# Attention features projected in pairs: seven block products, half of K ahead of the delta heads and half behind them

## The chip, the cores and the metric

One core of one Trainium2 chip runs the kernel. The metric is the device time of one execution in microseconds (us), the median of several runs. Five engines work side by side, each through its own list of instructions in a fixed order: TensorE (PE; its weight loads are shown apart as PEld), VectorE (DVE), ScalarE (ACT), GpSimd (POOL) and SyncE (SP), which only issues loads and stores. An instruction starts when the one before it on its engine is done with and when the semaphores it waits for have come.

## The reference

One encoder layer over 768 tokens, 512 of a prompt and 256 of a sample, which share the weights but do not see each other. The model width is 2048, and everything is float32.

```python
h = rms_norm(x, norm_g)
proj = h @ w_in            # 8192 features and 32 small columns
aq, ak, av, ag, dq, dk, dv, dg, b_raw, a_raw = split(proj)
attn = dilated_attention(aq, ak, av) * silu(ag)          # 8 heads x 128
qkv = silu(short_conv(concat(dq, dk, dv)))               # five taps over the tokens
dn = rms_norm(delta(fwd) + delta(bwd)) * silu(dg)        # 8 heads x 128
y = rms_norm(x + concat(attn, dn) @ w_out, final_gain)
```

Half of the 64 tiles of 128 features (`aq`, `ak`, `av`, `ag`) belong to attention, the other half to the delta heads. Each head of attention needs its q, k and v whole; each delta head its convolved q, k and v.

## The kernel before

**Exact products.** Float32 products are made from short parts: a tile `w` is split into `hi` (a cast on ScalarE) and `lo = w - hi` (a subtraction on VectorE or GpSimd; `w_split`, line 304), x likewise (`x_split`, line 401). A product is then hi·xh + hi·xl + lo·xh, three matmuls with the same shapes into one PSUM bank.

**Input projection.** `project` (line 470) does one tile of 128 features for all tokens: 16 K tiles, three products, each as a matmul of 512 prompt columns and one of 256 sample columns (`kstep`, line 321). The 64 tiles make 6144 matmuls `mm`. The x in them is not normalised: rows of x carry only the gain, and each tile's result is multiplied by `rB`, the reciprocal root mean square of every token, as it leaves PSUM. So the first product needs the first K tile of x, and not the mean over all of them. `x_squares` (line 411) adds the squares of x up, thirteen of the sums on GpSimd, and `start_rms` (line 554) makes `rB` by two matmuls `rms` with a matrix of ones. Beside the first tile run the small columns a and b (`ab_step`).

**Order.** Engines run written lists. A `Driver` makes them when the kernel is built: it keeps a rough clock of each engine, emits the projection's products one after the other, and after each product offers a place (`slot`, line 171) for up to three steps of side tasks whose inputs are due by those clocks. Delta heads (`prep`, `merge`, `chain`, `head_out`) and attention heads (`attend`, line 1007) are such side tasks; `drain` emits whatever side tasks are left, with nothing between them. Feature tiles come in this order: q, k, v of the delta heads with their gates, then q, k, v of each attention head with its gate behind it. The last four gates of attention (`LATE = 4`) stand behind the last head's q, k and v, so that products are left to go between the steps of the last heads.

**One head of attention.** `attend` works by 128 queries: S (scores, three matmuls per query tile), a VectorE row that adds the table of biases and takes the maximum, exp on ScalarE, the scaling on VectorE, transposes T, a split into high and low parts on ScalarE and VectorE, and at the end the product o with V. Prompt (four query tiles of 512 keys) and sample (two of 256) follow each other, and heads follow each other.

**Output projection.** The mixed features go through DRAM (`mixD`), are loaded back and split (`m_load`, `m_splits`), and multiplied with `w_out` in matmuls `mmo` of 512 columns (`ostep`).

The profile names lines of helpers: 192 is every instruction of VectorE, ScalarE and GpSimd, 272 every matmul, 277 every transpose, 234 every load and store.

## Time and profile before

| | |
|---|---|
| median of 3 runs | 1665.43 us (1664.51 to 1665.91) |
| span of the profiled execution, first to last instruction | 1662.0 us |
| PE busy | 1615.9 us, 97% |
| DVE, ACT, POOL busy | 841.0, 736.3, 416.3 us |
| mean granted clock of TensorE | 0.995 |
| moved by DMA | 150.32 MB |

The profiled execution is known by its span; its time as the runs count it is not listed. The median lies 3.4 us above the span, and by that much a span is brought to a time below. Busy times of PE count modelled ends of pipelined matmuls, so the pace of matmuls is read from start to start. "Idle before" is what an engine stood still ahead of an instruction, and the name behind the arrow is what it waited for.

### The profile page before, as it was taken

Reading aid. Unit: us, or ns where it says so; the run is one execution under the profiler, and the core shown is the slowest. Engines: PE = TensorE matmul, PEld = TensorE weight load, DVE = VectorE, ACT = ScalarE, POOL = GpSimd, SP = SyncE. Lnnn points to the kernel's source line nnn. Section 1 sums busy time; section 2 is a strip of 40 time slices with the busy share of each in tenths; the row PEclk is TensorE's granted clock in tenths of the full one; section 3 lists DMA queues with packets and bytes.
Section 4 is the critical chain, followed back from the end, with each engine's and each line's share of the span. In section 5 each row is a group of like instructions: output and inputs, shape, how many; then the busy total and the mean of one; then the engine's idle time right before and its main releaser. Section 6 shows DMA issues by size and latency. Waiting matters only on the chain.

```text
span 1662.0 us, 27562 instructions
## 1 busy us (share of the span) xinstructions
PE 1615.9 (97%) x10283; PEld 1392.2 (84%) x10283; DVE 841.0 (51%) x1956; ACT 736.3 (44%) x1861; POOL 416.3 (25%) x430
## 2 busy tenths in 40 slices
PE   5999999999999999999999999999999999999997
PEld 4788788888888888898888888888888888888885
DVE  6758674857677767675343342425334336313132
ACT  5575546564765566553433232424333335202121
POOL 4443413232424242332121222222121210111100
PEclk9999999999999999999999999999999999999999
DMA  5232312232323232313212222221221256534365
GB/s 190 61 89 72 97 47 79 64 87 59 83 62 87 65 80 65 87 47 84 67 49 79 65 61 69 61 75 55 78 75 57 72 188 224 158 91 118 90 200 180
DMA packets 107783, 150.32 MB, mean 90 GB/s; under 512 B 40864, under 2 KB 48128, under 8 KB 107648
## 3 DMA queue, kind: packets, MB, share of 16 engines
q1 hardware_dynamic: 105632, 143.83, 29.8%
q10 hardware_dynamic: 2016, 4.72, 0.7%
q8 instruction: 81, 1.33, 0.3%
q14 instruction: 54, 0.44, 0.1%
HBM read 125.65 MB, written 22.86 MB: 89 GB/s over the span
## 4 chain that ended last, share of the span: by engine, by line
PE 78%; DVE 9%; DMA 5%; ACT 4%; issue 3%; SPq 1%; POOL 0%; DVEq 0%; POOLq 0%; ACTq 0%
PE mm L272 55%; PE mmo L272 11%; PE c L272 5%; DVE lop L192 2%; PE o L272 2%; PE S L272 2%; DMA res<-in_x 1%; PE m L272 1%; DVE tmp L192 1%; PE kk L272 1%; PE T L277 1%; DMA xst<-in_xT 1%; DVE cacc L192 1%; DMA st<-in_wt 1%; DVE PB L192 1%
## 5 line engine op out<-in xcount | busy, mean ns | idle before, releaser
L272 PE MATMUL mm<-xl_x,hip 128*128 128x512 f32 (+1 forms) x2048 | 541.4, 345 | 7.6 <-DVE xl_x L192 7.6
L272 PE MATMUL mm<-xh_x,hip 128*128 128x512 f32 (+1 forms) x2048 | 538.0, 344 | 8.8 <-ACT hip L192 7.7
L272 PE MATMUL mm<-xh_x,lop 128*128 128x512 f32 (+1 forms) x2048 | 539.5, 345 | 0.0
L192 POOL TENSOR_TENSOR lop<-st,hip 128x256 fp32r<-128x256 f32 x252 | 205.8, 817 | 817.7 <-ACT hip L192 744.9
L272 PEld LDWEIGHTS mm<-xh_x,hip 128*128 128x128 f32 x2048 | 315.1, 189 | 52.2 <-ACT hip L192 8.1
L272 PEld LDWEIGHTS mm<-xl_x,hip 128*128 128x128 f32 x2048 | 315.9, 190 | 49.3 <-DVE xl_x L192 9.2
L272 PEld LDWEIGHTS mm<-xh_x,lop 128*128 128x128 f32 x2048 | 316.6, 190 | 41.4
L192 ACT CAST hip<-st 128x256 fp32r<-128x256 f32 x512 | 202.0, 402 | 328.0 <-PE mm L272 254.3
L192 DVE TENSOR_TENSOR lop<-st,hip 128x256 fp32r<-128x256 f32 x260 | 146.9, 566 | 323.7 <-ACT hip L192 313.4
L272 PE MATMUL mmo<-oh,xh_m 128*128 128x512 f32 x384 | 151.7, 395 | 0.4 <-DVE yt_a L192 0.4
L272 PE MATMUL mmo<-ol,xh_m 128*128 128x512 f32 x384 | 151.7, 395 | 0.0
L272 PE MATMUL mmo<-oh,xl_m 128*128 128x512 f32 x384 | 151.6, 395 | 0.0
L192 DVE TENSOR_TENSOR PB<-PB,tmp 88x30 f32<-88x30 f32 (+14 forms) x240 | 91.4, 381 | 8.2
L192 DVE TENSOR_TENSOR tmp<-PB 88x30 f32<-88x30 f32 (+14 forms) x240 | 92.2, 384 | 6.1 <-ACT PB L192 1.5
L272 PEld LDWEIGHTS mmo<-oh,xh_m 128*128 128x128 f32 x384 | 72.4, 189 | 17.6 <-DVE yt_a L192 0.9
L272 PEld LDWEIGHTS mmo<-ol,xh_m 128*128 128x128 f32 x384 | 72.4, 189 | 16.8
L272 PEld LDWEIGHTS mmo<-oh,xl_m 128*128 128x128 f32 x384 | 72.5, 189 | 16.7
L192 DVE TENSOR_TENSOR yt<-mmo,res 128x512 f32<-128x512 f32 x18 | 12.4, 690 | 126.9 <-PE mmo L272 92.6
L192 POOL TENSOR_TENSOR cacc<-cacc,ctmp 128x772 f32<-128x772 f32 x32 | 58.9, 1841 | 58.3 <-ACT ctmp L192 54.2
L192 ACT ACTIVATE s<-s,m 128x512 f32<-128x512 f32 (+1 forms) x48 | 31.3, 653 | 92.8 <-DVE m L192 92.8
L192 POOL TENSOR_TENSOR yt<-yt,fg 128x512 f32<-128x512 f32 x18 | 23.2, 1291 | 190.5 <-ACT res L192 190.5
L192 ACT ACTIVATE res<-yt 128x512 f32<-128x512 f32 x18 | 11.4, 632 | 132.7 <-DVE yt L192 132.7
(198 smaller groups left out, 1880.7 us busy)
## 6 DMA issues: line engine op xcount, KB each, us to landing
st<-in_wt SPq DMA_DIRECT2D x256, 256.0 KB
ost<-in_wo SPq DMA_DIRECT2D x32, 512.0 KB
dec<-gcD SPq DMA_DIRECT2D x24, 256.0 KB
xl_m<-mixD SPq DMA_DIRECT2D x16, 384.0 KB
res<-in_x SPq DMA_DIRECT2D x24, 256.0 KB
out_y<-row SPq DMA_DIRECT2D x12, 512.0 KB
xst<-in_xT SPq DMA_DIRECT2D x15, 384.0 KB
yD<-yt SPq DMA_DIRECT2D x18, 256.0 KB
```

The lines of the kernel that those rows point to most:

```text
L192: r = f(*a, **k)
L272: r = PE.matmul(out, lhsT, rhs, start=start, stop=stop)
L277: r = PE.transpose(out, in_, ident)
```

## The change

The 32 attention tiles are taken as 16 pairs: q and k of a head (8 pairs), two v tiles (4), two gates (4). For a pair the weights form blocks A (two tiles of features by two quarters of K) and x forms blocks B (two quarters of K by two halves of the tokens, 384 each). In place of eight block products there are seven (Strassen's, in Winograd's form): sums of blocks of weights S1 to S4 and of x T1 to T4 go in, and sums of results come out. One block product is 4 K tiles of three matmuls of 384 columns, so half of K of a pair takes 7 x 4 x 3 = 84 matmuls of 384 columns, where two tiles took 2 x 8 x 3 = 48 of 512 and 48 of 256.

The first half of K (`ph` 0) of all 16 pairs comes ahead of the delta heads' tiles, the second (`ph` 1) behind them. The first halves' results go to DRAM (`pD`, 64 stores of 192 KB) and come back (`part_load`), to be added on GpSimd. Weights are split 512 columns at a time (before: 256).

Since S and T mix rows of x with rows of another K quarter, x is normalised before it is used: the first pass (`project_raw`) does two delta gates and the a and b columns at once with raw x, a third gate follows, then `normalise` rewrites each K tile of x (`norm`) and makes the T sets (`block_sums`); those of the second half go to DRAM and come back during the last delta tile (`second_set`). Results no longer need `rB`. The q, k, v and gates of attention, and the gates of the delta heads, go through DRAM. Sample and prompt part of a head are separate tasks, and heads are spawned with the second halves of the pairs. The last pair (gates 6 and 7) comes after `drain`, in the pool of the output projection.

```diff
+PRODUCTS = {1: ("A11", "X", "B11"), 2: ("A12", "X", "B21"), 3: ("S4", "Z", "B22"), 4: ("A22", "Y", "T4"),
+            5: ("S1", "Z", "T1"), 6: ("S2", "Y", "T2"), 7: ("S3", "Y", "T3")}
+ORDER, FIRST_ORDER = (1, 6, 5, 2, 7, 3, 4), (1, 2, 5, 6, 3, 7, 4)
...
+            def plan_pair(pi, ph, order):
...
+                            V.tensor_tensor(out=s["S1"], in0=a("A21"), in1=a("A22"), op=ALU.add)
+                            V.tensor_tensor(out=s["S2"], in0=s["S1"], in1=a("A11"), op=ALU.subtract)
+                            V.tensor_tensor(out=a("A21"), in0=a("A11"), in1=a("A21"), op=ALU.subtract)
...
+                            V.tensor_tensor(out=s["S4"], in0=s["S4"], in1=s["S2"], op=ALU.subtract)
...
+                        r = w_split(src, f"p{m}", G if pr in (1, 5, 7, 3) else V)
...
+            def pair_products(pi, ph, order, kind, hook=None):
...
+                for n, pr in enumerate(order):
+                    _, b, name = PRODUCTS[pr]
+                    drv.until(lambda: there(ph, name))
...
+                    for i in range(4):
+                        v = inputs(ph, name, i)
+                        c = slice(i * P, i * P + P)
+                        for m, (w, j) in enumerate(((hi, 0), (hi, 1), (lo, 0))):
+                            mm(x["banks"][b][:, :HALF], w[:, c], v[j], start=(new and i == 0 and m == 0), stop=(i == 3 and m == 2),
+                               more=True)
...
+                    spawn(evacuate(x, pr), -20)
...
+            def norm(k, place=None):
+                yield from wait(lambda: rawdone[0] > k)
+                if k < 8:
+                    xn = xstage[k]
+                    V.scalar_tensor_tensor(out=xn, in0=xn, scalar=g_in[:, k:k + 1], in1=rB, op0=ALU.mult, op1=ALU.mult)
+                else:
+                    xn = st(place, (T,), f"xn{k}")
+                    V.tensor_tensor(out=xn, in0=xh[k].bitcast(F32), in1=xl[k].bitcast(F32), op=ALU.add)
+                    V.tensor_tensor(out=xn, in0=xn, in1=rB, op=ALU.mult)
+                xtiles(k, "n")
+                A.copy(xh[k], xn)
+                (V if k % 2 else G).tensor_tensor(out=xl[k], in0=xn, in1=xh[k].bitcast(F32), op=ALU.subtract)
...
+            def block_sums(i, xa, xb, room, end):
...
+                for n, (a, b) in {"T1": (xa[:, hi], xa[:, lo]), "T2": (xb[:, hi], "T1"), "T4": (xb[:, lo], "T2"),
+                                  "T3": (xb[:, hi], xa[:, hi])}.items():
...
+                    V.tensor_tensor(out=t[n], in0=a, in1=t[b] if isinstance(b, str) else b, op=ALU.subtract)
...
+                    A.copy(d[:, lo], t[n])
+                    (V if n in ("T1", "T3") else G).tensor_tensor(out=d[:, hi], in0=t[n], in1=d[:, lo].bitcast(F32), op=ALU.subtract)
...
+            project_raw((raw_gate_post(0, "f768"), raw_gate_post(1, "PBT")), raw_hook)
+            spawn(normalise(), -8)
...
+            project(58, raw_gate_post(2, "PB"), count)
+            for pi in range(NP2):
+                pair_products(pi, 0, ORDER if pi else FIRST_ORDER, kinds[pi])
...
+            for n, (f, post) in enumerate(single):
+                project(f, post, change if n == len(single) - 1 else None)
+            for h in range(NH):
+                spawn(halves(h, "q"), 10 * h + 99)
+                spawn(halves(h, "k"), 10 * h + 99)
+                spawn(attend(h), 10 * h + 100)
...
+            for n, pi in enumerate(second[:-1]):
+                pair_products(pi, 1, ORDER if n else FIRST_ORDER, kinds[pi], parts_hook)
+            drv.drain()
```

Three places of the order show what it moves. The first is on TensorE: the two `rms` matmuls. In the kernel before they stand among the products of the second feature tile, behind the whole pass that reads the raw x for a and b (`mm_0_480` and `mm_1_481` are that second tile's two banks):

```order
L272 MATMUL mm_0_480<-xh_x_144,lop_394 128x512
L272 MATMUL mm_1_481<-xh_x_144,lop_394 128x256
L272 MATMUL rms_510<-xacc,mgl 128x512
L272 MATMUL rms_513<-xacc,mgl 128x256
L272 MATMUL mm_0_480<-xh_x_159,hip_392 128x512
```

With the change they stand inside K tile 12 of the raw pass of two gates (`mmr1` is the second gate, `raw` its weights), and K tiles 13 to 15 come behind them:

```order
L279 MATMUL mmr1_0_128<-xh_x12_439,raw13_457 128x512
L279 MATMUL mmr1_1_129<-xh_x12_439,raw13_457 128x256
L279 MATMUL rms0_560<-xacc_98,mgl_528 128x512
L279 MATMUL rms1_563<-xacc_98,mgl_528 128x256
L279 MATMUL mmr1_0_128<-xl_x12_440,raw13_457 128x512
L279 MATMUL mmr1_1_129<-xl_x12_440,raw13_457 128x256
```

Products of the raw pass thus stand behind the sum of all squares, on the same engine. The second place is TensorE in the first pair: product 1 and 2 (bank X) read normalised x, product 5 (bank Z) reads the T1 of all four K tiles, the last of which (`T1s3`) is made last:

```order
L279 MATMUL mmX0_0_795<-xh_n7_832,hip21_762 128x384
L279 MATMUL mmX0_0_795<-xl_n7_833,hip21_762 128x384
L279 MATMUL mmX0_0_795<-xh_n7_832,lop21_763 128x384
L279 MATMUL mmZ0_0_921<-tset0_0_843,hip22_801 128x384 x2
...
L279 MATMUL mmZ0_0_921<-T1s3_913,hip22_801 128x384 x2
L279 MATMUL mmZ0_0_921<-T1s3_913,lop22_802 128x384
L279 MATMUL mmY0_0_946<-tset0_0_843,hip23_836 128x384 x2
```

Rows between the first and the last T1 are left out above. The third place is TensorE around the last heads. In the kernel before, products of a gate (`mm28`, `mm29`) stand behind each query tile of head 7:

```order
L272 MATMUL S7_3_14364<-khi7_14031,qklo7_13821 128x512
L272 MATMUL mm28_0_14156<-xl_x15_435,hip487_14271 128x512
L272 MATMUL mm28_1_14157<-xl_x15_435,hip487_14271 128x256
L272 MATMUL mm28_0_14156<-xh_x15_434,lop487_14273 128x512
L272 MATMUL mm28_1_14157<-xh_x15_434,lop487_14273 128x256
L272 MATMUL mm29_0_14377<-xh_x0_124,hip488_14298 128x512
```

With the change the last product of pair 14 (`mmY14`) stands ahead of the last query tile of head 5; the rest of head 5 and the whole of heads 6 and 7, 79 rows, follow without a product, and then comes pair 15:

```order
L279 MATMUL mmY14_1_14235<-xl_t7_10823,lop352_14325 128x384
L279 MATMUL S5_3_14432<-khi5_13655,qhi5_13641 128x512
...
L279 MATMUL S6_0_14516<-khi6_14174,qhi6_14139 128x512
...
L284 MATMUL T6_0_0_14560<-ident_526,s6_0_14520 128x128 x4
...
L279 MATMUL S7_0_14682<-khi7_14539,qhi7_14536 128x512
...
L279 MATMUL o7_0_14803<-PTh7_14679,Vl7_14666 128x512 x3
L279 MATMUL mmX15_1_14835<-xh_n8_995,hip353_14361 128x384
```

Of those 79 rows five are shown; the others are of the same kinds.

## Rows read from the trace of the kernel before

**Rows 1.** The page's head: the span, then busy us, share and instructions of each engine.

```profile
span 1662.0 us, 27562 instructions
PE 1615.9 (97%) x10283; PEld 1392.2 (84%) x10283; DVE 841.0 (51%) x1956; ACT 736.3 (44%) x1861; POOL 416.3 (25%) x430
```

**Rows 2.** The chain that ended last, share of the span by engine.

```profile
PE 78%; DVE 9%; DMA 5%; ACT 4%; issue 3%; SPq 1%; POOL 0%; DVEq 0%; POOLq 0%; ACTq 0%
```

**Rows 3.** Timeline of PE at 707 us: start, length, engine, line, operation, tiles, shape, count.

```profile
707.02 0.51 PE L272 MATMUL mm<-xh_x,lop 128*128 128x512 f32 x2
...
708.08 0.52 PE L272 MATMUL mm<-xh_x,lop 128*128 128x512 f32 x2
```

**Rows 4.** Timeline of PE at 1213 us: scores of a sample query tile.

```profile
1213.84 0.28 PE L272 MATMUL S<-khi,qhi 128*128 128x256 f32 x1
1213.96 0.27 PE L272 MATMUL S<-qklo,qhi 128*128 128x256 f32 x1
```

**Rows 5.** Waits of PE: what it waited for, us in total, times, longest.

```profile
PE mm L272 <- ACT hip L192: 7.7, 2, 7.3
...
PE mm L272 <- DVE xl_x L192: 7.6, 5, 3.1
PE ab L272 <- DVE hab L192: 4.2, 1, 4.2
```

**Rows 6.** Timeline of the first 60 us: VectorE, GpSimd and the rms matmuls.

```profile
9.87 1.02 DVE L192 SCALAR_TENSOR_TENSOR xl_x<-xst,g_in,xh_x 128x768 fp32r<-128x768 f32 x1 [1.65 <-ACT xh_x L192]
...
21.84 8.82 POOL L192 TENSOR_TENSOR xacc<-xacc,xst 128x768 f32<-128x768 f32 x4
...
24.49 2.58 DVE L192 SCALAR_TENSOR_TENSOR xl_x<-xst,g_in,xh_x 128x768 fp32r<-128x768 f32 x1
...
55.63 2.38 DVE L192 TENSOR_TENSOR xacc<-xacc,xst 128x768 f32<-128x768 f32 x2
...
58.06 1.56 PE L272 MATMUL rms<-xacc,mgl 128*128 128x512 f32 x4
```

**Rows 7.** Groups by line and form: busy us, mean ns of one, idle before.

```profile
L192 POOL TENSOR_TENSOR lop<-st,hip 128x256 fp32r<-128x256 f32 x252 | 205.8, 817 | 817.7 <-ACT hip L192 744.9 <-PE mm L272 57.2 <-PE c L272 7.4
L192 DVE TENSOR_TENSOR ol<-ost,oh 128x512 fp32r<-128x512 f32 x64 | 42.6, 716 | 17.4 <-ACT oh L192 17.2
L192 POOL TENSOR_TENSOR xacc<-xacc,xst 128x768 f32<-128x768 f32 x13 | 28.1, 2161 | 24.6 <-ACT xst L192 24.0
L192 POOL TENSOR_TENSOR yt<-yt,fg 128x512 f32<-128x512 f32 x18 | 23.2, 1291 | 190.5 <-ACT res L192 190.5
L192 POOL TENSOR_TENSOR qklo<-aq,qhi 128x768 fp32r<-128x768 f32 x8 | 14.7, 1841 | 18.9 <-ACT qhi L192 15.6 <-PE T L277 3.2
```

**Rows 8.** Windows: from:to and length, busy us of PE, PEld, DVE, ACT, POOL, PEclk, DMA.

```profile
60.00:100.00 40.00, 39.67 (x235) 34.33 (x234) 22.34 (x49) 24.56 (x59) 10.88 (x16) 1.00 0.28 79
...
178.00:182.00 4.00, 4.00 (x16) 3.43 (x15) 3.51 (x7) 0.99 (x3) 3.06 (x5) 0.57 0.67 196
...
800.00:1340.00 540.00, 538.19 (x3120) 471.00 (x3119) 202.27 (x507) 192.10 (x476) 112.59 (x124) 1.00 0.23 67
```

**Rows 9.** Timeline of one attention head, from its first transpose to its prompt output.

```profile
1183.68 0.60 PE L277 MATMUL av<-ident,av 128*128 128x128 f32 x4
...
1187.47 0.40 PE L272 MATMUL S<-khi,qhi 128*128 128x512 f32 x1
...
1188.37 0.69 DVE L192 CUSTOM_DVE_ANT_0 s<-S,tab 128x512 f32<-128x512 f32 x1 [1.26 <-PE S L272]
...
1190.98 0.49 DVE L192 TENSOR_SCALAR s<-s,m 128x512 f32<-128x512 f32 x1
...
1196.01 0.56 DVE L192 TENSOR_TENSOR PTl<-T,PTh 128x384 fp32r<-128x384 f32 x1 [0.60 <-ACT PTh L192]
...
1212.99 0.59 ACT L192 COPY ou<-o 128x512 f32<-128x512 f32 x1 [2.13 <-PE o L272]
```

**Rows 10.** Timeline of PE at 177 us, behind a wait in the first delta head.

```profile
176.99 1.10 PE L272 MATMUL kk<-kq 128*128 128x256 f32 x4 [4.00 <-DVE in L192]
```

More of the change, by code (lines that the diff above doesn't have):

```diff
@@ L332, in encoder_kernel @@
         A.mul(warm, eps_t, 1.0)
-        rB = cp.tile([P, T], F32, name="rB")
+        sums3 = [wp.tile([P, HALF], F32, name=f"sum{i}") for i in range(3)]
         with tc.tile_pool(name="sp", bufs=1) as sp:
@@ new lines, in over, with prepare @@
+            def over(n):
+                dead.add(n)
+                stages.pop(n)
+            def prepare(upto):
+                while cur["made"] <= min(upto, len(plan) - 1):
+                    m = cur["made"]
+                    size, last, make = plan[m]
+                    feed()
+                    if last >= cur["load"] or live and cur["w"] + size - 6 > min(live.values()):
+                        assert m > cur["used"]
+                        break
+                    live[m] = cur["w"]
+                    made[m] = make(m)
+                    cur["w"] += size
+                    cur["made"] += 1
+                feed()
@@ new lines, in target @@
+            def target(x, side, half):
+                if not x["ph"]:
+                    yield from get("dec")
+                    return st("dec", (HALF,), f"part{x['pi']}_{side}{half}")
+                if x["kind"] == "last":
+                    return last_target(x, side, half)
+                if side not in x["asked"]:
+                    x["asked"].add(side)
+                    yield from get("f768")
+                    x["out"][side] = f768(f"out{x['pi']}_{side}")
+                else:
+                    yield from wait(lambda: side in x["out"])
+                return x["out"][side][:, half * HALF:(half + 1) * HALF]
@@ L525, in post @@
                 def post(ps):
-                    yield from wait(lambda: "rms" in flags)
                     yield from get("cin", "cacc")
@@ L554, in start_rms @@
             def start_rms():
-                yield from wait(lambda: len(xsq) == 0 and emitted["x"] == NK and drv.ready(xacc))
+                yield from wait(lambda: sq[0] == NK and drv.ready(xacc))
                 for h in (0, 1):
@@ L991, in split, with halves @@
                 E.tensor_tensor(out=lo, in0=src, in1=hi.bitcast(F32), op=ALU.subtract)
[L993 removed]
+            def halves(h, what):
+                yield from wait(lambda: (what, h) in stored)
                 place = "ktok" if what == "k" else "AT"
@@ L1097, in attend, with put_out @@
                     yield 0
-                give("attend", "AT", "ktok", "vtok", "vtok", "kq", "XT")
-                if h >= NH - LATE:
-                    AQ.dma_start(ouD[h - NH + LATE], ou)
-                    give("oacc")
-                    return
-                yield from wait(lambda: f"a{h}" in gates and drv.ready(gates[f"a{h}"]))
-                g = gates.pop(f"a{h}")
+                done.append(t0)
+            heads, mixed = set(), set()
+            stored = set()
+            def put_out(kind, h, t, to):
+                if kind == "g":
+                    A.activation(t, t, AF.Silu)
+                    yield 0
+                SY.dma_start(to, t)
+                stored.add((kind, h))
+                give("f768")
+                yield 0
```

654 lines of the change are left out of this document (463 added, 191 removed).

## Prediction

> **What bounds the kernel now.** I read the page's head first: PE is busy for 97% of 1662.0 us [rows 1], and the chain of waits lies on PE for 78% [rows 2]. So the kernel is a stream of matmuls, and any other engine matters only where PE waits for it. The timeline gives the stream's pace: between 707.02 and 708.08 us three groups of one 512 and one 256 column matmul start, 0.353 us a group [rows 3]. Scores of 256 columns, each with a weight load of its own, start 0.115 us apart [rows 4]. I take 0.349 us a group (0.232 and 0.117), so one feature tile costs 48 x 0.349 = 16.75 us. Next the waits of PE: its long ones lie at the start, for the first `hip`, the splits of x and the small columns' split, 19.5 us in all [rows 5]; after 60 us it hardly stops (39.67 of 40 us) [rows 8]. In the attention stage PE is busy for 538 of 540 us while DVE has 202 and POOL 113 us of work there [rows 8]: heads are hidden behind products. One head takes its time, 29.9 us from its first transpose to its prompt output at 1213.58 [rows 9], but PE goes on meanwhile.
>
> One thing off PE matters for this change. Alone, a 768 column split of x takes DVE 1.02 us; beside an addition of POOL it takes 2.58 us, while four POOL additions take 8.82 us together [rows 6]. DVE rows that read two SBUF tiles and POOL rows run nearly one at a time, so their times have to be added.
>
> **The saving.** Half of K of a pair takes 84 matmuls of 384 columns in place of 48 x 0.349 = 16.75 us. No row shows 384 columns. The nearest rows bound it: 0.117 us (9.8 us) and 0.232 us (19.5 us). The straight line between them gives 0.1745 us, and I take it because 0.117 is almost exactly half of 0.232: what is paid is paid by the column. That is 14.66 us, 2.09 less, and 32 such halves give **-67 us**; a line off by 2 ns would move this by 5. The ends would give -222 and +88 us, far from what a line through two points allows. For back-to-back matmuls the Trainium skill, "TensorE: Matmul & The Clock Gate", section "Back-to-back issue gap", states N/2.4 + 2.5 ns, 162.5 ns at 384 columns; the trace has 232 where it gives 215.7 ns at 512, so the row decides, and by the page the saving would be 99 us.
>
> **The start.** The matmuls `rms` need the sum of all squares. In the kernel before, DVE's last two additions to it begin at 55.63 and `rms` at 58.06 [rows 6], but `rms` stands behind the first tile and four K tiles of the second; PE does not care. With the change `rms` stands inside K tile 12 of the raw pass. Shared DVE and POOL work up to there, from the order: 16 splits of x (1.02 us), 10 `lo` of 256 (0.42, half of a 512 row plus a fixed part [rows 7]), 5 squares, 2 sums and the small columns' split (7.7), 28 us on DVE; 13 sums of 768 (1.84, as the undisturbed `qklo` [rows 7]; in the first 60 us they average 2.16) and 6 `lo` (0.75), 28 us on POOL. That is 57 us and begins near 5 us: `rms` at **61 us**, though PE comes to it near 42. Behind it stand 3.7 K tiles of 2.8 us; the pass ends at 73 at full clock, 75 with the half clock that a long wait leaves (below). Only then are the gates copied, multiplied by `rB` on DVE and the norms started behind them: 79. Eight norms, first sums of weights and splits are 17 us on DVE and 11 on POOL: 107. PE meanwhile does tile 58 until 92 and product 1 and 2, then waits. Each T set is four subtractions of 384, two `lo` on DVE and two on POOL, 5.2 us; T1 of the fourth comes after three sets and 1.5 us, at 124. Behind it stand five products of 12 x 0.1745 us, with their clock loss: pair 0 ends at 135. The matmuls up to there (three tiles 50.3, a and b 11.2, pair 14.7) are 76 us. The kernel before has 32 us of such work behind it at 58 us (first tile 16.75, a and b 11.2, four K tiles of the second), does `rms` in 1.2 and runs on [rows 8]: it is through with 76 at 103. **+32 us** (20, if half of the shared work overlaps, to 45, if each step is as late as the longest rows say).
>
> **Pairs 1 to 6.** Beside them go the second half's norms and T sets (48 us of shared work by the prices above) and their own weights: 4 sums and 3 `lo` of 512 on DVE (0.69 each) and 4 `lo` on POOL (1.29 [rows 7]), 10 us a pair. With 107 us of shared work beside 92 of PE these pairs run at DVE's and POOL's pace: **+12 us** (3 to 20). From pair 7 on it is 10 against 14.7: nothing, hidden by PE with 4 us to spare. The 29 delta tiles keep their side work, and `lo` stays as it was in columns: nothing.
>
> **Loads and stores.** 64 stores and 64 loads of partial results, 32 of T, and q, k, v and gates through DRAM are some 69 MB beside 150 (sizes from the order), on SP in front of weight loads. The DMA engines are busy 0.23 to 0.28 of the time [rows 8], and weights are loaded ahead into five places, about two products' time beyond the split in hand; that hides them: nothing. If a store that waits for its result held a weight load for longer than that, each such case would cost PE 1 to 2 us; this lies in the range of the next two terms.
>
> **Pairs with attention.** A pair's half with its share of a head is about 19.5 us of PE and 16 of DVE, 10 of POOL, and results wait for sums from `pD`. Before, DVE was busy for 37% of this stage [rows 8]; now some 80%, in short waits: **+5 us** (0 to 25).
>
> **The bare heads.** By the order the rest of head 5 and heads 6 and 7 stand behind the last product of pair 14, and pair 15 behind them. A head's matmuls are 9.9 us: six S, 20 transposes of 0.11, 18 products o, six av. From the rows of one query tile: S at 1187.47, its maximum 1188.37, the scaling done 1191.47 with a DVE row between, transposes, and the last split near 1197.2 [rows 9]. Without products and delays such a chain is 5.8 us; DVE's share of it is 2.4 us, and two tiles are under way at once, so a prompt tile follows another after 2.7 to 2.9 us. Four, their start, o and the sample's two tiles make 21 to 23 us a head. With 11 us of head 5 and two loads of a bias table (each behind the head ahead of it) it is 57 to 65 us, of which 24 are PE's work and were paid before: **+36 us**. At least DVE's own 13.6 us a head, +9; at most one query tile after the other as in [rows 9], +53.
>
> **Clock and seam.** After the wait of 4.00 us at 177 the granted clock is 0.57 for 4 us [rows 8, 10], half speed, some 2 us lost. The bare stretch and the wait behind it bring two more such: **+4** (0 to 15). The output weights' loads stand on SP behind the last heads' outputs, and in a busy DVE: **+4** (0 to 8).
>
> **Sum.** -67 + 32 + 12 + 5 + 36 + 4 + 4 = +26 us on the span of 1662.0; the median stands 3.4 above the span, so **1692 us**, slower. A measurement here tells some 0.2% (3 us) from no change.
>
> **Rivals.**
> *DVE and POOL overlap after all (faster).* Place: raw pass, first norms, pairs 1 to 6. If each engine's own 28 us were the bound, the sum of squares would be there by 48 us, pair 0 through by 108, pairs 1 to 6 bound by PE: the two terms fall from 44 to about 5, and the time to 1653. It decides from about 26 us of these 44 on. Against it stand the stretched rows [rows 6]. A milder form is likelier than the full one: 0.18.
> *Heads overlap at the end (no change).* If the heads' steps ran at DVE's own pace, +9 in place of +36: 1665. Against it: S and T stand in turns on PE, and heads take turns. 0.1.
> *All is hidden.* Only the saving is left: 1598. It asks that `rms` be ready when PE comes, against rows and order: 0.03.
> *DVE bounds the attention half (slower still).* If its 80% with waits for sums becomes 100%, 15 pairs lose 2.5 us each, +38 in place of +5: 1725. 0.14.
> *384 columns cost less than the straight line.* At 0.1625 us, 7% under it, a half takes 84 x 0.1625 = 13.65 us and saves 3.1: -99 in place of -67, so 1660. The rows at both sides, which lie on one line through nearly nothing, speak against it: 0.02. (It is the price of the section of the Trainium skill named above.)
>
> **How the numbers follow.** My forecast has 0.53, with a range of its own of 1672 to 1712. Taking the first rival's 1653, the second and most of the fourth in, the range is 1645 to 1725. Faster by over 0.2%: the first, third and last rival and some of the second and of the forecast's low side, 0.27; within 0.2%: 0.07; slower: 0.66.
>
> **What would show it.** Right: matmuls of 384 start 0.17 us apart; `rms` near 61 us with PE idle before it; a wait of 20 us or more ahead of product 5 of pair 0, whose end is near 135; some 60 us between the last `mmY14` and the first `mmX15`, with PE under half busy in them. Wrong: `rms` before 50 us, pair 0 through by 115, or PE busy while heads 6 and 7 run; then the time lies below 1665.

## The result and the profile after

The changed kernel takes **1860.27 us**, median of 4 runs (1856.52 to 1864.62), against 1665.67 us for the kernel before on the same chip (1664.51 to 1667.25): a ratio of 1.117 (95% interval 1.115 to 1.119), 195 us slower where +26 was forecast. The profiled execution spans 1856.7 us.

The head of the page, with the slices that show where PE stood still, and the first numbers of the chain of waits:

```profile
span 1856.7 us, 27423 instructions
PE 1631.0 (88%) x9899; PEld 1436.6 (77%) x9899; DVE 1066.8 (57%) x2129; ACT 821.9 (44%) x1864; POOL 559.9 (30%) x436
...
PE   7747889999989999999999978898889658899997
...
DVE  7577776544657577557757474576677645332032
...
PEclk9867999999999999999999998999999877999999
...
PE 20%; DVE 6%; ACT 3%; DMA 3%; issue 2%; POOL 1%; SPq 1%; ACTq 0%; POOLq 0%; DVEq 0%
```

Against [rows 1, 2]: PE did 97% of the span and is down to 88%, with 384 matmuls fewer. The chain lay on PE for 78%, and now its shares add up to some 36%: it could be followed back only so far, and PE is little more than half of what was followed. DVE has 226 us more work, POOL 144. The mean granted clock fell from 0.995 to 0.94. A slice is 46 us. Three places show: slices 3 and 4 (the start), slices 24 to 31 (pairs with attention), slices 32 and 33 (the bare heads). The delta stage between them looks full, though it is not.

The same in windows, with the columns of [rows 8]:

```profile
100.00:200.00 100.00, 65.33 (x285) 58.74 (x286) 72.76 (x110) 34.50 (x68) 34.35 (x25) 0.75 0.21 70
300.00:400.00 100.00, 100.00 (x574) 100.00 (x573) 55.78 (x82) 34.93 (x62) 41.14 (x28) 1.00 0.39 130
411.00:1103.00 692.00, 654.14 (x4914) 569.63 (x4913) 436.89 (x1042) 401.51 (x1032) 205.19 (x174) 0.98 0.26 77
1103.00:1470.00 367.00, 312.96 (x1877) 292.19 (x1877) 234.78 (x501) 155.16 (x345) 149.18 (x115) 0.94 0.52 174
1470.00:1549.00 79.00, 41.90 (x153) 31.05 (x152) 36.88 (x106) 30.55 (x70) 1.85 (x1) 0.70 0.27 95
```

From 300 to 400 us the change does what it is meant to: 574 matmuls in 100.00 us, 0.174 each. The next row is the delta tiles, then pairs with attention, then the bare stretch. In the pairs with attention PE stands still for 54 of 367 us (367 less 312.96), and a granted clock of 0.94 there means some 44 us at the lower of its two levels. DVE is at 64% (234.78 of 367), not the 80% that I expected; a sum of work does not bound that stage.

What PE waited for (us in total over the whole span, times, longest):

```profile
PE mmY L279 <- DVE out L199: 29.3, 6, 7.3
PE mmX L279 <- ACT sum L199: 20.9, 5, 10.3
PE T L284 <- DVE s L199: 20.8, 11, 4.4
PE tr L284 <- ACT kq L199: 12.1, 5, 5.3
PE mmY L279 <- DVE part L199: 11.2, 5, 3.6
PE mmr L279 <- ACT xh_x L199: 10.7, 1, 10.7
PE rms L279 <- DMA mgl<-in_cst: 9.4, 1, 9.4
```

Each is a few waits of 2 to 10 us, of many kinds. Two I had not thought of: `mmY <- out` (a result tile) and `tr <- kq` (a delta head).

Where the time went, by stages. "Lost" is elapsed time less the matmuls at the pace they have when they run on (a pair's half 14.67 us, other kinds by their usual distance from start to start), so it holds waits and half clock alike. It counts from the first matmul, and that one comes 3.4 us later with the change (10.73 against 7.34), which the first difference includes:

| stage of the changed kernel | elapsed, us | lost | lost before, same work | difference | predicted |
|---|---|---|---|---|---|
| to the store that ends pair 0, 147.6 | 147.6 | 55 | 20 | +38 | +32 |
| pairs 1 to 6, to 287.3 | 139.7 | 43 | 0 | +43 | +12 |
| pairs 7 to 15, to 410.7 | 123.4 | 0 | 0 | 0 | 0 |
| delta stage, to 1103.2 | 692.5 | 69 | 32 | +37 | 0 |
| second halves, heads and seam, to the first `mmo` at 1569.8 | 466.6 | 139 | 3 | +136 | +49 |
| products saved | | | | -67 | -67 |

In the stage of the second halves, 16 halves of 14.67, eight heads of 9.9 and some 14 us of the last delta head are 328 of the 466.6 us of PE. The differences sum to +187; the first `mmo` comes 187.2 us later than before (1569.8 against 1382.6), and the rest of the 194.7 us lies behind it, in an output projection that takes 286.9 in place of 279.4 us. The lost times are counts from many rows, good to a few us each. By the same count the 139 us are some 80 in the pairs with attention, 54 in the bare stretch and 6 in the last pair.

### The profile page after: what moved, and what is told of

It is laid out like the page before. It is cut to its first block, busy times and chain, and to the rows that moved or that the text cites. A ratio compares the mean times of both kernels' runs of the same rounds, so it can differ in the third digit from the quotient of the medians.

```text
span 1856.7 us, 27423 instructions
## 1 busy us (share of the span) xinstructions
PE 1631.0 (88%) x9899; PEld 1436.6 (77%) x9899; DVE 1066.8 (57%) x2129; ACT 821.9 (44%) x1864; POOL 559.9 (30%) x436
## 5 line engine op out<-in xcount | busy, mean ns | idle before, releaser
L199 POOL TENSOR_TENSOR lop<-st,hip 128x512 fp32r<-128x512 f32 x156 | 224.2, 1438 | 550.5 <-ACT hip L199 459.9
L199 ACT CAST hip<-st 128x512 fp32r<-128x512 f32 x280 | 171.5, 617 | 186.9 <-PE mm L279 58.2
L279 PE MATMUL mm<-xh_n,lop 128*128 128x512 f32 (+1 forms) x928 | 249.1, 350 | 0.0
L279 PE MATMUL mm<-xl_n,hip 128*128 128x512 f32 (+1 forms) x928 | 248.7, 349 | 0.0
L279 PE MATMUL mm<-xh_n,hip 128*128 128x512 f32 (+1 forms) x928 | 248.2, 349 | 0.0
L199 DVE TENSOR_TENSOR lop<-st,hip 128x512 fp32r<-128x512 f32 x124 | 103.9, 838 | 188.2 <-ACT hip L199 177.4
L279 PEld LDWEIGHTS mm<-xh_n,lop 128*128 128x128 f32 x928 | 144.3, 192 | 17.8
L279 PEld LDWEIGHTS mm<-xl_n,hip 128*128 128x128 f32 x928 | 144.3, 192 | 17.7
L279 PEld LDWEIGHTS mm<-xh_n,hip 128*128 128x128 f32 x928 | 144.1, 192 | 17.4
L279 PE MATMUL mmX<-xh_n,hip 128*128 128x384 f32 x256 | 90.0, 352 | 20.9 <-ACT sum L199 20.9
```

The costliest lines, as they stand in the source:

```text
L199: r = f(*a, **k)
L279: r = PE.matmul(out, lhsT, rhs, start=start, stop=stop, skip_group_check=more)
```

## The experiments

My first theories of the last stage: **A**, DVE is the bound there, since GpSimd's rows hold it up and `lo` adds to both; **B**, result tiles stand in places that are not free in time; **C**, one serial start feeds everything; **D**, the chain of a head's steps. They were tried apart first. Most experiments are a single run; intervals are given where a kernel ran several times. The four runs of the changed kernel lie 8 us apart (1856.52 to 1864.62), and the first product of the second halves starts anywhere from 1098.2 to 1103.7 us in runs that leave all work before it alone, so a single difference of less than some 8 us is not told from none. Each edit also moves the `Driver`'s rough clocks, so the lists are written anew: what an edit does to an engine and what it does to the order are tried together. "Row of heads" below is the time from the first stored head output (`ouD<-ou`) to the eighth.

**All low parts of weights on DVE.**

```diff
-                    plan.append((2, len(loads) - 1, make(len(loads) - 1, G if c % 2 else V)))
+                    plan.append((2, len(loads) - 1, make(len(loads) - 1, V)))
...
-                        r = w_split(src, f"p{m}", G if pr in (1, 5, 7, 3) else V)
+                        r = w_split(src, f"p{m}", V)
```

> All lo parts of the projection's weights (188 of 512 columns that stood on GpSimd) are made on VectorE. Theory A (VectorE and GpSimd rows exclude each other, so the sum of their work sets the pace of the pairs and stretches the delta stage): 188 x (1.44 - 0.72) = about 135 us less of shared work, of which a third to a half lies on TensorE's path: 1780 to 1820 us, the delta stage (from the last bare pair to the first load of partial results) shrinks from 700 to about 680 us. Theory B (VectorE's queue stands still behind stores into places that are used again, and TensorE behind VectorE): VectorE has more to do and its waits stay: 1840 to 1880 us.

1865.83 us, nothing won, as B had it. But the parts moved: the delta stage fell from 692.5 to 673.1, as A had it, and pairs with attention and the bare stretch grew by 31. `lo` matters in both stages, with opposite signs.

**A second place for result tiles.** The two results of a pair used two places of one name (`f768`), which gates of delta heads use too; one goes to the place of the convolution's temporary, unused by then.

```diff
-                    yield from get("f768")
-                    x["out"][side] = f768(f"out{x['pi']}_{side}")
+                    if side:
+                        yield from wait(lambda: len(convs) == 24)
+                    yield from get(("f768", "ctmp")[side])
+                    x["out"][side] = st(("f768", "ctmp")[side], (T,), f"out{x['pi']}_{side}")
...
```

> The second tile of each attention pair's result gets a place of its own (that of a convolution tile no longer used), so results no longer take turns with gates and reloaded q and k in one pair of places. Theory B: the six waits of TensorE for VectorE's result rows (29 us in the second halves' stage) mostly go, and with them the half clock behind them: 1815 to 1835 us. Theory A: these waits are only where VectorE's lateness shows; others take their place: 1850 to 1865 us.

1834.59 us, -26; the pairs with attention fell from 367.5 to 347.6. What such a wait looked like in the changed kernel, on DVE and then on PE:

```profile
1195.77 1.13 DVE L199 SCALAR_TENSOR_TENSOR gate<-tro,dng,gate 128x512 f32<-128x512 f32 x2
1203.60 0.56 DVE L199 TENSOR_TENSOR out<-mmX,xh_n 128x384 f32<-128x384 f32 x1 [6.70 <-DMA mixD<-gate]
...
1206.42 0.98 PE L279 MATMUL mmY<-xh_t,hip 128*128 128x384 f32 x2 [7.25 <-DVE out L199]
```

The result tile's place was last held by a delta gate. It is free only when that gate's store to `mixD` has landed; DVE stands 6.70 us, and PE behind it 7.25. DVE's head rows stood in the same queue. With the second place, in the list of PE's waits:

```profile
PE mmY L279 <- DVE out L199: 11.9, 6, 3.7
```

**The start's shared work on DVE alone**: sums of squares, `lo` of raw weights, `xl_n` and the T sets' low parts.

```diff
-                        (V if k >= NK - 2 else G).tensor_tensor(out=xacc, in0=xacc, in1=t, op=ALU.add)
+                        V.tensor_tensor(out=xacc, in0=xacc, in1=t, op=ALU.add)
...
-                (V if k % 2 else G).tensor_tensor(out=xl[k], in0=xn, in1=xh[k].bitcast(F32), op=ALU.subtract)
+                V.tensor_tensor(out=xl[k], in0=xn, in1=xh[k].bitcast(F32), op=ALU.subtract)
...
```

> GpSimd's share of the start (13 sums of squares, 6 lo parts of the raw weights, 8 low parts of normalised x, the T sets' low parts) is done on VectorE. Theory A: each such row costs half as long there and the two engines' sum is what counts: the shared work of the raw pass falls from 57 to about 43 us, but the constants that the rms matmuls also need land only at 62.8 us, behind weight loads, so the rms matmuls stay near 60; norms and T sets lose 15 to 20 us in all: pair 0 ends near 135 in place of 144, pair 7 near 270 in place of 295, total 1830 to 1840 us. If each engine's own work set the pace, VectorE would be later: pair 7 ends at 305 or more, 1865 to 1880 us.

1840.52 us, -20: `rms` at 50.0 in place of 62.9, pair 0 through at 141.2, pair 6 at 260.2 in place of 287.3. With GpSimd left out, the same work is done sooner by one engine than by the two: the sum of squares is through at 49.3 in place of 59.5. I had expected `rms` to stay near 60, held by the load of its matrix of ones; but that load stands behind weight loads that wait for the same shared work, and it was issued at 43.8 in place of 59.5.

**The three together.**

> The three edits together. Theory A and B both hold: the gains add, 1740 to 1780 us. If only A holds: 1760 to 1810; if only B: 1830 to 1880. In every case heads 6 and 7 still stand without products, some 75 us long, so it stays slower than the kernel before.

1825.37 us (ratio 1.097, 1.094 to 1.100): 35 us gained of the 46 that the second and third gave alone, between the ranges that I had given. The bare stretch grew to 105 us, as it grew with the first edit alone.

**Product 7 earlier in a pair**, so that the bank `mmY` is read sooner.

```diff
-ORDER, FIRST_ORDER = (1, 6, 5, 2, 7, 3, 4), (1, 2, 5, 6, 3, 7, 4)
+ORDER, FIRST_ORDER = (1, 6, 5, 7, 2, 3, 4), (1, 2, 5, 6, 3, 7, 4)
```

> The seven products of a pair in the order 1, 6, 5, 7, 2, 3, 4 in place of 1, 6, 5, 2, 7, 3, 4: two products of 2.1 us in place of one stand between product 7 and product 4, which adds to the bank that VectorE must have read after product 7; in turn one product in place of two stands between 6 and 7. Theory B2 (TensorE waits in the middle of a pair because one product is too little cover for a VectorE queue that runs late): the waits of bank Y for results shrink, 15 to 30 us less: 1830 to 1845 us. Rival (VectorE is late by more than two products, wherever the reading stands): the waits move to product 7, 1850 to 1880 us.

1854.07 us, inside the scatter: pairs 19 us shorter, the bare stretch 15 longer. A wait of products removed came back behind the last product. That was the first sign that products do not set the end of this stage.

**Low parts of the delta tiles alone on DVE** (the first line of the first experiment).

> Only the delta tiles' lo parts (58 of 512 columns on GpSimd) go to VectorE; those of the pairs stay. If the 512 column rows of GpSimd are what stretches the delta stage (theory A): that stage shrinks by some 20 us, as with all of them moved, and the attention stage keeps its 367 and 78 us: 1835 to 1845 us. If the stage's extra time has another cause: 1855 to 1865 us.

1838.96 us, -21, nearly all of it from the delta stage (672.8). Groups of instructions that bear on it; first the changed kernel, then this one, then the kernel before (columns of [rows 7]):

```profile
L199 POOL TENSOR_TENSOR lop<-st,hip 128x512 fp32r<-128x512 f32 x156 | 224.2, 1438 | 550.5 <-ACT hip L199 459.9 <-PE c L279 29.8 <-DVE oa L199 11.5
...
L199 DVE SCALAR_TENSOR_TENSOR cacc<-cin,cw,cacc 128x772 f32<-128x772 f32 x64 | 72.5, 1132 | 15.8 <-ACT cacc L199 14.9
```

```profile
L199 DVE SCALAR_TENSOR_TENSOR cacc<-cin,cw,cacc 128x772 f32<-128x772 f32 x64 | 66.2, 1035 | 4.7 <-ACT cacc L199 4.2
```

```profile
L192 DVE SCALAR_TENSOR_TENSOR cacc<-cin,cw,cacc 128x772 f32<-128x772 f32 x64 | 67.5, 1055 | 3.1 <-ACT cacc L192 2.7
```

A `lo` of GpSimd now lasts 1438 ns in one piece, where it was 817 [rows 7]. The convolution's row on DVE took 1132 ns on average, and takes 1035 without those pieces; it was 1055 beside the shorter pieces before. These rows alone are 6 us; PE's wait for a delta head's `kq`, which is made from them, fell from 12.1 to 1.7 us. No run leaves the `lo` on GpSimd in two pieces of 256, so that the width is the cause is argued from these rows and not shown apart. The Trainium skill, "SBUF — State Buffer", section "Who interferes with whom", states that DVE and GpSimd contend for one shared port pair, an exclusive lock; the stretched rows (1132 against 1035 ns) agree.

**Another place for T1's temporary**, for pairs 1 to 6.

> The T1 block, which is held through a whole T set, gets a place of its own, so that partial results and the other T blocks have three places in place of two. Theory B (VectorE stands still behind stores to places used again, 12.6 us of waits for stores in the first pairs): pairs 1 to 6 shrink by 10 to 20 us, 1838 to 1850 us. Theory A (shared work of VectorE and GpSimd sets their pace): 0 to 4 us, 1855 to 1862 us.

1860.64 us, no difference. Pair 6 ends 7 us earlier, and it is lost again later.

**Matmuls that nobody reads, in the steps of heads 6 and 7**, to hold the clock (`fill(6)` makes six of them).

```diff
...
+                        fill(6)
                         s = st("dec", (512,), f"s{h}_{t}")
...
+                        fill(6)
```

> Matmuls that nobody reads (6 of 512 columns behind each query tile's scores and behind its transposes, heads 6 and 7, prompt part) keep TensorE at work in the stretch without products. Its output is the reference's. If the half clock makes a good part of that stretch (mean granted clock 0.70 over 78 us): 8 to 12 us less, 1846 to 1852 us. If only the chain through VectorE and ScalarE counts: within 2 us of 1858, or more where the added matmuls stand ahead of the chain's own.

1850.35 us, -10. The bare stretch in a window (in the changed kernel it is the last window above, 79.00 us at clock 0.70):

```profile
1465.50:1541.00 75.50, 55.30 (x246) 43.30 (x246) 36.48 (x105) 30.28 (x70) 1.87 (x1) 0.86 0.28 98
```

The clock rose to 0.86 and the stretch shrank by 3 us; most of the rest is an earlier start of the stage (1098.2 against 1103.2), which lies in the scatter named above. So little of the 10 us is the clock's: the half clock is a small part of the bare stretch, and the chain of steps is the large one.

**Low parts of products 6, 2 and 4 of the second halves on GpSimd.** By A this makes the stage worse, by D better.

```diff
-                        r = w_split(src, f"p{m}", G if pr in (1, 5, 7, 3) else V)
+                        r = w_split(src, f"p{m}", G if ph or pr in (1, 5, 7, 3) else V)
```

> In the second halves of the pairs the three lo parts that VectorE makes (48 rows of 512) go to GpSimd as well. Theory D (in the attention stage VectorE's own queue is the bound: each head is a chain that passes it some ten times a query tile, in turns with the pairs' sums): VectorE has 48 x 0.8 = 38 us less of 281, the stage of 466 us (pairs, stretch without products, last pair) falls to 440 to 455, total 1830 to 1850 us. Theory A (the sum of VectorE's and GpSimd's rows is the bound, and GpSimd's take twice as long): 29 us more of shared work, the stage rises to 475 to 490, total 1865 to 1885 us.

1825.25 us, -35, against A and below the range of D. In the window of the pairs with attention GpSimd does 42 us more than in the changed kernel, DVE 27 less:

```profile
1105.00:1470.00 365.00, 314.87 (x1889) 294.89 (x1888) 207.34 (x494) 161.61 (x369) 191.10 (x153) 0.93 0.51 170
```

The stream of products even got longer (pairs 367.5 to 379.7 us), while the bare stretch fell from 78.3 to 32.8. D reads this so: what counts is how soon a row of a head comes up in DVE's queue. The order changed with it, though: of the 144 score matmuls 39 stand behind the last product of pair 14 in the changed kernel, and 18 here. No run holds the order fixed, so how much of the gain is the queue's and how much the order's stays open.

**Scaling of the softmax on ScalarE**, to take a row off DVE.

```diff
-V.tensor_scalar(out=s[:, :w], in0=s[:, :w], scalar1=m[:, 3:4], scalar2=None, op0=ALU.mult)
+A.mul(s[:, :w], s[:, :w], m[:, 3:4])
```

> The scaling of each query tile's weights by its sum (48 rows of 0.5 to 1.0 us in the attention stage) goes from VectorE to ScalarE, which is busy for 42% of that stage. Theory D: VectorE loses 25 to 30 us of 281, the stage of 466 us falls by 10 to 25, total 1832 to 1847 us. If the lock with GpSimd or the stores to places used again are what counts there, the total stays within 6 us: 1851 to 1863 us.

1876.08 us, +16, a miss for both theories. DVE has less to do, but the step waits in ScalarE's queue: PE's wait for `s` is 24.0 us, now on ACT, in place of 20.8 on DVE.

**No scores, softmax or product with V.**

> Leaves out the scores, the softmax and the product with V of all eight attention heads (each head's output is its q); the pairs, their loads and stores and the gates stay. It shows what the pairs' second halves cost without heads: 15 of 14.67 us on TensorE are 220 us, with the rest of the delta heads about 250. If the heads' rows in VectorE's queue are the cause of the stage's waits (theory D): 250 to 275 us from the first product of the second halves to the last pair, total near 1640. If the pairs' own sums and reloads hold TensorE back (theory B: places, stores and loads): 300 us and more, total 1680 or more.

1745.66 us, -115; some 74 us of that are the heads' own matmuls (the transposes of v stay). The fifteen halves still take 313 us where 220 is their pace (15 x 14.67); D had 250 to 275, B 300 and more. So products have waits of their own here, not caused by heads, and nearly as large as with heads: PE stands still for 49 of 313.5 us and the granted clock is 0.92, against 54 of 367 and 0.94. The window, and what PE waited for from 1100 us on:

```profile
1099.50:1413.00 313.50, 264.58 (x1604) 256.47 (x1602) 178.65 (x290) 110.13 (x213) 154.69 (x116) 0.92 0.65 213
```

```profile
PE mmY L279 <- DVE out L199: 32.3, 7, 7.8
...
PE mmX L279 <- ACT sum L199: 8.8, 1, 8.8
PE mmZ L279 <- DVE sum L199: 3.9, 1, 3.9
```

From the first product of the second halves to the first `mmo` it is 354.0 us where PE's work is some 254, so 100 are lost; with heads it is 466.6 for 328, so 139 are lost.

**Five changes together**: place, start, delta `lo`, scaling on ScalarE, unread matmuls.

> The edits of the place of its own for results, the start on VectorE, the delta tiles' lo parts on VectorE, the scaling on ScalarE and the matmuls that nobody reads in the last two heads, together. If their single gains add (26, 20, 20, 8 and 10 to 25 us): 1755 to 1780 us. If the heads' chain sets the length of the attention stage, a part is lost again there: 1780 to 1800 us. Either way slower than the kernel before.

1821.36 us (ratio 1.094, 1.092 to 1.096). That is outside both ranges, and again far less than the sum of the parts (20, 26, 21 and 10 us won, 16 lost). The second place shortened the pairs (346.8), but the bare stretch is 101 us, and the whole stage takes 466.3 us as in the changed kernel.

That led to theory **E**: the eight heads are one row, each begins when the one before has stored its output, and this row, not the amount of products, ends the stage. E asks that products can be added at no cost.

**Product 1 of fifteen second halves done twice**: 31.4 us more of matmuls.

```diff
-                    for i in range(4):
+                    for i in (0, 1, 2, 3, 0, 1, 2, 3) if ph and pr == 1 and kind != "last" else range(4):
```

> In the second halves of 15 pairs the first product is made twice (180 matmuls of 384 columns more, 31.4 us of TensorE; the first of the two results is overwritten). Theory E (the attention stage is as long as eight heads in a row, some 44 us each from one head's end to the next, and the products only fill it): the pairs' part grows and the stretch without products shrinks by nearly as much; the total rises by 0 to 12 us, 1857 to 1870. If the products' own pace and waits set the length: plus 28 to 35 us, 1885 to 1895.

1844.4 us: 31 us of work more, 16 us *less*, below both ranges. Stores of head outputs (eight, first and last start), in the changed kernel, in this one, with the second halves' low parts on GpSimd, and with the second place for results:

```profile
L241 ACTq DMA_DIRECT2D ouD<-ou x8: 326/326/344, 1249.2 to 1549.8; - x8
```

```profile
L241 ACTq DMA_DIRECT2D ouD<-ou x8: 326/327/344, 1231.5 to 1536.1; - x8
```

```profile
L241 ACTq DMA_DIRECT2D ouD<-ou x8: 326/326/389, 1235.1 to 1516.8; - x8
```

```profile
L241 ACTq DMA_DIRECT2D ouD<-ou x8: 326/327/390, 1229.9 to 1525.8; - x8
```

E holds in what it asked: PE's amount of work is not the bound. The row of heads is 300.6 us for seven steps in the changed kernel, 43 us a head on average, and 304.6 with the added products. Five of the stores of the changed kernel, for the length of single heads, which is 43 to 46 us beside products and 35 and 27 us in the bare stretch:

```profile
1384.76 0.33 ACTq L241 DMA_DIRECT2D ouD<-ou  x1
...
1429.18 0.33 ACTq L241 DMA_DIRECT2D ouD<-ou  x1
1487.89 0.33 ACTq L241 DMA_DIRECT2D ouD<-ou  x1
1523.12 0.33 ACTq L241 DMA_DIRECT2D ouD<-ou  x1
1549.83 0.33 ACTq L241 DMA_DIRECT2D ouD<-ou  x1
```

The span ends 307 us behind the eighth output in each: 1856.7 - 1549.8, 1842.7 - 1536.1, 1823.5 - 1516.8, 1832.8 - 1525.8. It does so, within 306 to 310, in all runs that have heads, because pair 15 and the output projection are written behind the last head. So two numbers decide: when the first head is through, and how long the row is. The first is 146 us into the stage in the changed kernel (1103.2 to 1249.2), and the products' waits lie in it; 129 with the second place. What starts the row earlier comes through whole: the start on DVE moves the first output to 1230.1 (-19, time -20), the delta tiles to 1227.2 (-22, time -21). Low parts and scaling change the row itself: 319.7 us with all `lo` on DVE (1237.2 to 1556.9), 317.1 with the scaling on ScalarE, 281.7 with the second halves' `lo` on GpSimd. Why the first head came 18 us sooner beside longer products stays open; the order is written anew around them, with places for steps after each added product and 12 score matmuls behind the last product in place of 39. Nor does E say that products alone would be fast: without heads their own waits remain. The two stand side by side. Where the pairs got shorter and the first head no sooner (all five changes: 21 us shorter, the first output 146 us into the stage), the bare stretch took it back; with the second place alone the pairs won 20 us, the first output came 17 us sooner, and the stage fell by 22. No run lets two heads overlap, and none takes the heads out with the second place in, so how far each alone would reach was not tried.

**The convolution's input copied by DVE**, added to the delta tiles' `lo`.

```diff
-A.copy(Z["cin"][:, o:o + width[h]], ps[h][:, :width[h]])
+V.tensor_copy(out=Z["cin"][:, o:o + width[h]], in_=ps[h][:, :width[h]])
```

> As the run with the delta tiles' lo parts on VectorE, and besides the convolutions' input is copied from PSUM by VectorE, as before, in place of ScalarE. If ScalarE's queue holds the delta chain (its waits appear before TensorE's transposes): the delta stage shrinks from 673 to 655 to 665 us. If VectorE's queue does: 675 to 690 us.

1836.81 us. The delta stage falls from 672.8 to 666.9, between the two ranges; some 11 us of its loss stay open. The total is 2 us less, which a single run does not tell from none.

**The usual order of products in the first pair of the second halves.**

> The first pair of the second halves takes the usual order of products in place of the special one, in which product 2 stands right behind product 1 and waits for ScalarE's copy of its bank (9 us, and 4 us behind it). The pair ends some 10 us sooner. Theory E: the first head can begin no sooner than the last delta head lets it, so little comes of it: 1850 to 1858 us; if the products set the length: 1842 to 1848 us.

1860.24 us, no difference; the first output comes at 1245.8, the last at 1549.7.

**What helps, together**: start on DVE, delta `lo` on DVE, second halves' `lo` on GpSimd, second place, unread matmuls.

> The start on VectorE, the delta tiles' lo parts on VectorE, the second halves' lo parts all on GpSimd, a place of its own for results and the unread matmuls in the last heads. Single gains 20, 20, 33, 26 and 8 us; the fourth and fifth overlap with the third, since all three shorten the same row of heads: 1765 to 1790 us. Still slower than the kernel before.

1770.27 us (ratio 1.064, 1.062 to 1.066), 90 us better than the change and the best that I found, in the range that I had given. It is still 6% slower than the kernel before. The row of heads is 266.9 us and begins 54 us earlier; the page, and the stores of head outputs:

```profile
span 1768.6 us, 27551 instructions
...
PE   7858889999999999999999998989999977999997
```

```profile
L241 ACTq DMA_DIRECT2D ouD<-ou x8: 326/332/395, 1194.9 to 1461.8; - x8
```

## Why the prediction was right or wrong

**The saving: right.** Stores of partial results of one pair's half follow the last pair's after 14.67 us (362.40, 377.07 and 391.74), 84 matmuls of 0.1746 us; I had 14.66. PE at 1186 us and the stores, each by its start and length:

```profile
1186.24 0.34 PE L279 MATMUL mmX<-xh_n,lop 128*128 128x384 f32 x1
1186.41 0.34 PE L279 MATMUL mmX<-xh_n,hip 128*128 128x384 f32 x1
1186.59 0.33 PE L279 MATMUL mmX<-xl_n,hip 128*128 128x384 f32 x1
```

```profile
362.40 0.38 SPq L241 DMA_DIRECT2D pD<-part  x1
...
377.07 0.38 SPq L241 DMA_DIRECT2D pD<-part  x1
...
391.74 0.38 SPq L241 DMA_DIRECT2D pD<-part  x1
```

Cheaper matmuls of 384 columns, a rival, did not come.

**The start: right in its steps, +38 for +32.** `rms` began at 62.94 (61), T1 of the fourth set was ready at 126.2 (124):

```profile
62.94 2.90 PE L279 MATMUL rms<-xacc,mgl 128*128 128x512 f32 x4 [9.40 <-DMA mgl<-in_cst]
...
126.26 1.28 PE L279 MATMUL mmZ<-T1s,hip 128*128 128x384 f32 x2 [3.60 <-ACT T1s L199]
127.34 0.52 PE L279 MATMUL mmZ<-T1s,lop 128*128 128x384 f32 x1
127.66 0.84 PE L279 MATMUL mmY<-tset,hip 128*128 128x384 f32 x2
```

One part I had not seen. The last of the sums was done by 59.5; what came last was the load of the ones, `mgl`, which stood on SP behind weight loads that waited for places:

```profile
46.98 12.03 SPq L241 DMA_DIRECT2D st<-in_wt  x5
...
59.54 0.42 SPq L241 DMA_DIRECT2D mgl<-in_cst  x1
```

The end of pair 0 is off (its last product starts near 144 and its last store at 147.6, for 135): from T1 on, the first matmuls run at half clock, 0.32 us apart in the rows at 127.34 and 127.66, product 4 waits 2.9 us until DVE has read its bank, and the granted clock of 100 to 200 us is 0.75.

**Pairs 1 to 6: +43 for +12, mis-sized.** About half of it is the cause I named: with the shared work on one engine, pair 6 came 27 us earlier, 21 of them in these pairs. I set the two engines' work of 107 us beside 92 of PE, which is +15 and not +12, and six halves are 88, which makes it +19; and I let PE run through the rest; it stood still for 28 of these 139.7 us at late rows of other engines, none of them a T set, and worked at half clock for another 28 (mean granted clock 0.90). Its longest waits in this stretch:

```profile
PE mmY L279 <- DVE part L199: 8.3, 4, 3.6
PE pgt L284 <- ACT scr L199: 5.2, 1, 5.2
```

How the 43 split into waits and clock was not tried apart.

**"The 29 delta tiles keep their side work, and `lo` stays as it was in columns: nothing": wrong, +37.** The columns stayed, the width of one instruction doubled (817 to 1438 ns on GpSimd), and DVE's rows beside it took longer; that this is how the time went is the likeliest reading, not a shown one. 20 us go away with these `lo` on DVE, 6 perhaps with the copies (no more than the scatter), some 11 are open.

**"Loads and stores: nothing": wrong.** I looked at bandwidth and at weight loads behind stores. What cost 26 us, of which 22 lie in the stage of the second halves, was a place that is free only when its store has landed, and the DVE row that waits for it, with heads and products behind.

**"Pairs with attention: +5", "bare heads: +36", "clock +4", "seam +4": +136 together for +49, and here lies most of the error.** The first failed as a step, some 80 us for 5: I weighed this stage as amounts of work, 80% of DVE, and put the waits between them at next to nothing. DVE did 64%, and PE still stood for 54 of 367 us and worked at the lower clock for some 44. The products' own results cost most of that, since without heads the loss is much the same (49 of 313.5 us): their places, free only when a store has landed, and the sums. On top of it heads run one behind the other, the first through 146 us into the stage and the next ones 43 to 46 us apart, so that what the products win counts only as far as the first head comes sooner. In [rows 9] I read 29.9 us for one head with PE going on; eight of those are 239 us, less than the 299 of PE beside them (220 of products and 79 of their own), so that row alone gave no warning. What the rows before could not show is that a head beside pairs takes 43 to 46 us. The wait that stretches it, in DVE's queue or in the order written around it, stays open. The bare heads were the right mechanism with a size too small: 78.3 us for 57 to 65. Some 47 of them pass at the lower clock (0.70 of 79), but a higher one (0.86) shortened them by 3 us only. One head alone lasted 35 and 27 us (heads 6 and 7, from output to output), not 21 to 23; the bias table's load, issued behind two loads that wait for the head before, is one of its waits:

```profile
1491.50 0.42 SPq L241 DMA_DIRECT2D tab<-in_tabs  x1
...
1496.65 0.69 DVE L199 CUSTOM_DVE_ANT_0 s<-S,tab 128x512 f32<-128x512 f32 x1 [6.76 <-DMA tab<-in_tabs]
```

**The rivals.** (The terms add up to 1691.4 and not 1692, which changes nothing.) That DVE and POOL overlap did not come true: the sum of squares was through at 59.5 us, where 48 had been the mark. Heads did not overlap at the end either. "DVE bounds the attention half" named the right stage and gave 1725; its reason, a DVE that is busy all the time, did not come (64%). DVE's queue counts all the same: the ninth experiment took 27 us of work off it and won 35. The side of the forecast (slower) was right, and start and bare heads were reasons for it; but most of the 195 us came from terms put at nothing or +5, whose upper ends had not been worked out from a chain of waits.

## What to carry to other kernels

When a change cuts the work that side tasks hide behind, count the side tasks as a row: steps in series times the length of one beside the new work, and when the first can begin. A busy share says nothing about it. Then take the side tasks out: what is still lost belongs to the main work. When an instruction is made wider on an engine that stretches another's rows, ask who stands behind it, though the sum of columns is the same. And for each place that is taken anew, ask what frees it: if that is a store, its landing belongs on the path.

## What the runs showed of the hardware that was not expected

- More matmuls made the kernel faster (31.4 us more work, 16 us less time): PE's amount of work was not the bound of its stage though it is 85% busy there in the changed kernel (312.96 of 367 us).
- One engine did the start's shared work sooner than two: the sum of squares was through at 49.3 us with GpSimd's part given to DVE, at 59.5 with both at work.
- The lower level of the clock follows waits of a few us: PE waited 4.58, 3.60 and 3.60 us between 111 and 126 us, and the matmuls of 384 columns at 127 stand 0.32 us apart, 0.1746 in the stream; the mean granted clock of the whole span is 0.94 for a kernel whose PE is 88% busy. For 384 columns at full clock, the Trainium skill, "TensorE: Matmul & The Clock Gate", section "Back-to-back issue gap", gives 162.5 ns, an estimate by its formula N/2.4 + 2.5; the trace has 174.6.
